# Layer 1's backward and output steps: SP in program order, z and x1 loads moved, squares written to SBUF

## The chip, the cores and the metric

One core of one Trainium2 chip runs the whole program. The metric is the device time of one execution in microseconds (us); the kernel before took 2016.53 us (median of three executions, 2014.89 to 2018.07). A change of 0.2%, some 4 us, is about what a measurement of this kernel can tell from none.

## What is computed

The reference is a two-layer backbone over 2048 latent tokens and 256 context tokens of width 1024. Layer 0 (chunked gating and windowed attention) is not touched. Layer 1 is a bidirectional gated linear recurrence and an output projection, followed by the final norm:

```python
z = depthwise_conv(xr, conv_w, conv_b)
for d, reverse in ((0, False), (1, True)):
    a_l, b_l = rglru_coeffs(z, w_a[d], b_a[d], w_i[d], b_i[d], lam[d])   # two sigmoid gates, exp, sqrt
    s_l = linear_scan(a_l, b_l, h0, reverse)
    h_lat = s_l if h_lat is None else h_lat + s_l
y = (h_lat * silu(g)) @ w_out
x = x + gate * y
return rmsnorm(x, final_g)
```

All products are made of three float32r products of high and low halves, so an operand is first split into such halves (on ScalarE and VectorE).

## The kernel before

The 18 tiles of 128 tokens go in 9 pairs (`L = NPAIR = 9`). Layer 1 is a software pipeline of steps `s` = 0 to 24, one call of `step(s)` each. A step does the recurrence work of one pair, which `gate(s)` names, in four blocks `b` of 256 channels, and the projection work of another pair, which `proj(s)` names, in four PSUM banks `b`:

- recurrence: forward direction in steps 3 to 11, backward direction in steps 12 to 20 (step 12 is the context pair, which stores no result);
- projection: `xr_mm` in steps 0 to 8, `g_mm` (the gate branch) in steps 9 to 16, `out_mm` (the output projection, the residual and the norm) in steps 17 to 24.

Within a step the order of ScalarE (ACT), TensorE (PE) and VectorE (DVE) is that of the code, since the loop stands in `tc.manual_schedule` for these three engines (L1422). GpSimd (POOL) and the sequencer SP, from which all DMAs are issued, are ordered by the scheduler, which emits what it finds ready.

The order of the code in a backward step `s`, as far as it matters:

1. `z_load(s)` (L1316): four loads `zf<-zs` of 256 KB, z of the next pair, into a ring of six buffers (L1206). Blocks 0 and 1 take buffers that the step before has done with. Blocks 2 and 3 take those of this step's own blocks 0 and 1, which POOL's product `ig<-ig,zf` (L1108) reads last.
2. `halves_load(s+1)`: four loads `op<-h1s` of 512 KB (until step 16).
3. for each block, `gmm` (PE, `pr` and `pig`) and `gates_act` (ACT sigmoids, L1106); between them the work left over from the step before (`tail`, which calls `post`) and `next_z(s, b)`: the split `zhl<-zf` of the next pair's z, ACT L84 and then DVE L87. Blocks 0 and 1 are split between the sigmoids, block 2 after all four and after `mm(0)`.
4. `coeff` (ACT L1125, DVE L1128 to L1132) of blocks 0 and 1, `next_z(s, 3)`, `mm(1)`, `coeff` of blocks 2 and 3, `root` (ACT L1136), `mm(2)`, `op_load(s+1, k)` (in steps 16 to 23, two loads of 512 KB).
5. `scan(d, i, (0, 1))`: DVE `r<-r,ig` (L1141), the scans (L1149), the sum with the forward result (L1158) and the product with the gate (L1160), then the store `y1s<-T` (L1164); `mm(3)`; `scan` of blocks 2 and 3 likewise.
6. `load_hg` (L1166): eight loads `hf<-hfs` and `gs<-gs` of 256 KB for the next pair's sums.

The sigmoid of block 0 writes the buffer of `r` that the scan of block 0 in the step before has read (ring of four). `hook` loads new weights `w<-kepto` of 1 MB each: the output weights `wo[2]` and `wo[3]` in step 17, behind `next_z(s, 2)`; banks 2 and 3 of that step need them.

In an output step, `post(b)` (L1230) adds the bank to the residual rows (DVE L1239) and takes the sum of squares on ACT, writing the squares back into the bank:

```python
dve.tensor_tensor(xt, xt, po, ALU.add)
act.activation(po, xt, AF.Square, accum_out=ss[:, half:half + 1])
if late:
    late.pop()()
```

so the bank is free for the next product when ACT L1240 is done. The residual rows `xt<-x1s` (256 KB a half) come into a ring of four buffers with the tag "gs", loaded in `post` when a tile's first half is met; the same buffers hold a tile's finished rows until the store `out<-xt` (`late`, L1266) has landed. `FG` rows, `og` and the ring "T" (four buffers of the scans) are the other buffers that the change names.

Of the kernel before, what the change touches and what calls it, by code (L numbers as in the profile page):

```python
# [7 lines left out]
F32 = mybir.dt.float32  # L8
F32R = mybir.dt.float32r
BF16 = mybir.dt.bfloat16  # L10
AF = mybir.ActivationFunctionType
# [4 lines left out]
P = 128  # L16
# [17 lines left out]
U_AT = 5  # L34
Y_ROWS = 1
T_PE = 14
MOD_AT = 8
WO1_AT = (2, 4, 6, 8, 10, 11, 12, 13)

# [2 lines left out]
def backbone_kernel(ctx: ExitStack, tc: tile.TileContext, a, out):  # L42
    nc = tc.nc
    pe, act, dve, pool, sp = nc.tensor, nc.scalar, nc.vector, nc.gpsimd, nc.sync
# [974 lines left out]
    L = NPAIR  # L1019
    order = [0] + list(range(L - 1, 0, -1))  # L1020

    with ExitStack() as c4:
# [185 lines left out]
        def g_mm(s, i, b):  # L1208
# [9 lines left out]

            return mm, post

        def out_mm(s, i, b):
            x, half = divmod(b, 2) if s > 2 * L - 1 else (b % 2, b // 2)
            t = 2 * i + x

            def mm():
                ps = px_tile()
                mm_wide(ps, wo[2 * half:2 * half + 2], lambda hl, c: ops[s, c][:, hl, x * P:(x + 1) * P])
                pxs[b] = ps

            def post():  # L1230
                if half == 0:
                    xts[t] = []
                    for h in range(2):
                        xt = b1.tile([P, 512], F32, tag="gs", name="xt", bufs=4)
                        sp.dma_start(xt, x1s[t][:, 512 * h:512 * h + 512])
                        xts[t].append(xt)
                    xts[t].append(b1.tile([P, 2], F32, tag="ss", name="ss", bufs=2))
                xt, ss, po = xts[t][half], xts[t][2], pxs.pop(b)
                dve.tensor_tensor(xt, xt, po, ALU.add)  # L1239
                act.activation(po, xt, AF.Square, accum_out=ss[:, half:half + 1])  # L1240
                if late:
                    late.pop()()
                end = s == 3 * L - 3 and x == 1
                if half == 0:
                    if end:
                        dve.tensor_tensor(xt, xt, FG[:, 0:512], ALU.mult)
                    return
                ms = b1.tile([P, 1], F32, tag="ms", name="ms", bufs=2)
                e = dve if end else pool
                if end:  # L1250
                    og = b1.tile([P, 512], F32, tag="G", name="og", bufs=1)
                    dve.tensor_tensor(og, xt, FG[:, 512:], ALU.mult)
                e.tensor_tensor(ms, ss[:, 0:1], ss[:, 1:2], ALU.add)
                e.tensor_scalar(ms, ms, 1.0 / D, EPS, ALU.mult, ALU.add)
                pool.tensor_tensor(ms, ms, mhalf[:, 0:1], ALU.pow)

                def final():
                    o = xts[t][:2]
                    if end:
                        o[1] = og  # L1260
                        act.activation(o[0], o[0], AF.Copy, scale=ms)
                        dve.tensor_scalar(og, og, ms, None, ALU.mult)
                    for h in range(2):
                        if not end:
                            dve.scalar_tensor_tensor(o[h], o[h], ms, FG[:, 512 * h:512 * h + 512], ALU.mult, ALU.mult)
                        sp.dma_start(out[0, (t - NCT) * P:(t - NCT + 1) * P, 512 * h:512 * h + 512], o[h])  # L1266

                late.append(final)

            return mm, post  # L1270
# [40 lines left out]
        def next_conv(s, b):  # L1311
            nx = gate(s + 1)
            if nx and nx[0] == 0:
                conv(nx[1], b)

        def z_load(s):  # L1316
            nx = gate(s + 1)
            if nx and nx[0]:
                for b in range(4):
                    sp.dma_start(z_tile(*nx, b), zs[nx[1]][:, 2 * b:2 * b + 2])  # L1320

        def step(s):
            g, M = gate(s), proj(s)

            def G(f, *args):
                if g:
                    f(*g, *args)
# [13 lines left out]
            def tail(b):  # L1341
                if len(tails) and tails[0][0] == b:
                    tails.pop(0)[1]()

            z_load(s)
            if s + 1 < 2 * L - 1:
                halves_load(s + 1)
            first = early(s) and s != 2 * L - 1
# [2 lines left out]
            G(gmm, 0)  # L1351
            G(gates_act, 0)
            tail(3)
            if early(s) and not first:
                op_split(s, 0)
            next_conv(s, 0)
            G(gmm, 1)
            G(gates_act, 1)
            if early(s):
                op_split(s, 1)  # L1360
            next_conv(s, 1)
# [32 lines left out]
            if source(s + 1) and s + 1 >= 2 * L - 1:  # L1394
                for k in range(2):
                    op_load(s + 1, k)
                    if not early(s + 1):
                        op_split(s + 1, k)
            if E:
                post(0)  # L1400
            G(scan, (0, 1))
# [14 lines left out]
        def early(s):  # L1416

            return 2 * L - 1 <= s <= 2 * L + 2
# [1 line left out]
        tails = []  # L1420
        step(0)
        with tc.manual_schedule(engines={mybir.EngineType.Activation, mybir.EngineType.PE, mybir.EngineType.DVE}):  # L1422
            for s in range(1, 3 * L - 2):
                step(s)
            for _, f in tails:
                f()
            late.pop()()
# [49 lines left out]
```

## Time and profile before

| | us |
|---|---|
| three executions, median (lowest to highest) | 2016.53 (2014.89 to 2018.07) |
| the profiled execution | 2019.23 |
| its span, first to last instruction | 2017.4 |
| matmuls busy in the span (PE) | 1903.2 (94%) |
| VectorE (DVE) busy | 1527.7 (76%) |
| ScalarE (ACT) busy | 1086.5 (54%) |
| GpSimd (POOL) busy | 619.8 (31%) |
| granted TensorE clock, mean | 0.974 |

PE is busy nearly all the time as a mean over the span, but the mean hides the stretch that the change touches: steps 12 to 24, which run from about 1571 us to the end. There the idle time of the weight loads (PEld) shows PE's waits, since matmuls are modelled as overlapping. A row of the timeline gives start, duration, engine, line, operation, tiles, count and in brackets the idle time of the engine before it with what ended it. "SPq" is the sequencer that issues DMAs: its duration is that of the issue, not of the transfer.

### The profile page before, as it was taken

Reading aid. Unit: us, or ns where it says so; the run is one execution under the profiler, and the core shown is the slowest. Engines: PE = TensorE matmul, PEld = TensorE weight load, DVE = VectorE, ACT = ScalarE, POOL = GpSimd, SP = SyncE. Lnnn points to the kernel's source line nnn. Section 1 sums busy time; section 2 is a strip of 40 time slices with the busy share of each in tenths; the row PEclk is TensorE's granted clock in tenths of the full one; section 3 lists DMA queues with packets and bytes.
Section 4 is the critical chain, followed back from the end, with each engine's and each line's share of the span. In section 5 each row is a group of like instructions: output and inputs, shape, how many; then the busy total and the mean of one; then the engine's idle time right before and its main releaser. Section 6 shows DMA issues by size and latency. Waiting matters only on the chain.

```text
span 2017.4 us, 33905 instructions
## 1 busy us (share of the span) xinstructions
PE 1903.2 (94%) x12159; PEld 1701.9 (84%) x12159; DVE 1527.7 (76%) x3223; ACT 1086.5 (54%) x2205; POOL 619.8 (31%) x801
## 2 busy tenths in 40 slices
PE   7999999999999899799989999999999999988998
PEld 3778888888887788688878889999999999877777
DVE  8878989786745787838888854798987566877863
ACT  6656656666655332323443551676767666756621
POOL 2745646454422311200010010443422121244310
PEclk8999999999999899899999999999999999988999
DMA  9355535352344897465555555324476464866442
GB/s 344 124 180 186 176 137 176 118 199 71 126 142 149 297 353 281 172 230 182 198 205 182 206 208 186 107 100 147 167 260 222 161 200 167 295 218 192 136 160 91
DMA packets 184788, 375.79 MB, mean 186 GB/s; under 512 B 18694, under 2 KB 78858, under 8 KB 176428
## 3 DMA queue, kind: packets, MB, share of 16 engines
q1 hardware_dynamic: 184620, 373.64, 53.0%
q8 instruction: 95, 1.56, 0.3%
q14 instruction: 73, 0.60, 0.1%
HBM read 246.41 MB, written 127.17 MB: 185 GB/s over the span
## 4 chain that ended last, share of the span: by engine, by line
PE 57%; DVE 19%; ACT 10%; DMA 7%; issue 6%; POOL 1%; SPq 1%; POOLq 0%; DVEq 0%; ACTq 0%
PE px L90 6%; PE px L92 6%; PE px L91 6%; DVE h1T L904 4%; PE pu L90 3%; PE pu L91 3%; PE pu L92 3%; PE po L573 3%; PE ptp L561 2%; DVE yT L904 2%; DVE macc L231 2%; ACT h1T L175 2%; DMA mraw<-in_w_mod 2%; PE pl L515 1%; PE pq L91 1%
## 5 line engine op out<-in xcount | busy, mean ns | idle before, releaser
L90 PE MATMUL px<-op,w 128*128 128x256 f32 x1088 | 308.1, 283 | 0.0
L91 PE MATMUL px<-op,w 128*128 128x256 f32 x1088 | 307.9, 283 | 0.0
L92 PE MATMUL px<-op,w 128*128 128x256 f32 x1088 | 307.9, 283 | 0.0
L91 PEld LDWEIGHTS px<-op,w 128*128 128x128 f32 x1088 | 208.9, 192 | 0.0
L90 PEld LDWEIGHTS px<-op,w 128*128 128x128 f32 x1088 | 208.9, 192 | 0.0
L92 PEld LDWEIGHTS px<-op,w 128*128 128x128 f32 x1088 | 208.9, 192 | 0.0
L543 POOL TENSOR_SCALAR s<-s,ri 128x640 f32<-128x640 f32 (+2 forms) x144 | 134.4, 947 | 97.1 <-DVE ri L540 93.0
L535 ACT ACTIVATE s<-s,mn 128x641 f32<-128x641 f32 (+2 forms) x144 | 113.3, 788 | 65.8 <-DVE mn L517 57.7
L84 ACT ACTIVATE pT<-ptp 128x512 fp32r<-128x512 f32 (+1 forms) x192 | 99.7, 536 | 89.5 <-PE ptp L561 86.4
L1108 POOL TENSOR_TENSOR ig<-ig,zf 128x512 f32<-128x512 f32 x72 | 109.9, 1534 | 98.0 <-ACT ig L1106 88.7
L87 DVE TENSOR_TENSOR zhl<-zf,zhl 128x512 fp32r<-128x512 f32 x72 | 60.2, 843 | 102.8 <-ACT zhl L84 102.7
L573 PE MATMUL po<-pT,v 128*128 128x256 f32 x656 | 130.1, 296 | 6.1 <-DVE pT L87 4.4
L87 DVE TENSOR_TENSOR pT<-ptp,pT 128x512 fp32r<-128x512 f32 (+1 forms) x192 | 114.4, 604 | 23.3 <-ACT pT L84 22.6
L90 PE MATMUL px<-w,op 128*128 128x512 f32 x256 | 103.5, 404 | 14.9 <-ACT px L1240 14.9
L573 PEld LDWEIGHTS po<-pT,v 128*128 128x128 f32 x656 | 98.5, 189 | 17.2 <-DVE pT L87 9.1
L175 ACT ACTIVATE h1T<-h1T,mc 128x128 f32<-128x128 f32 x112 | 44.7, 482 | 119.0 <-DVE h1T L904 119.0
L561 PE MATMUL ptp<-ident,s 128*128 128x128 f32 x656 | 104.0, 273 | 3.9 <-POOL s L543 2.1
L1152 POOL COPY carry<-T 128x2 f32<-128x2 f32 x68 | 34.7, 510 | 232.1 <-DVE T L1149 222.1
L904 DVE STREAM_TRANSPOSE h1T<-hrow 32x256 f32<-32x256 f32 x224 | 97.7, 436 | 8.1 <-ACT hrow L956 5.0
L91 PE MATMUL px<-w,op 128*128 128x512 f32 x256 | 102.5, 400 | 0.0
L92 PE MATMUL px<-w,op 128*128 128x512 f32 x256 | 102.4, 400 | 0.0
L517 DVE CUSTOM_DVE_ANT_0 s<-pl,mask,mn 128x384 f32<-128x384 f32 (+1 forms) x128 | 76.1, 594 | 31.5 <-PE pl L515 30.1
(280 smaller groups left out, 6237.4 us busy)
## 6 DMA issues: line engine op xcount, KB each, us to landing
hp<-h0s SPq DMA_DIRECT2D x45, 1024.0 KB
op<-h1s SPq DMA_DIRECT2D x64, 512.0 KB
mraw<-in_w_mod SPq DMA_DIRECT2D x48, 512.0 KB
h0s<-hT SPq DMA_DIRECT2D x18, 1024.0 KB
h1s<-h1hl SPq DMA_DIRECT2D x36, 512.0 KB
xt<-in_x SPq DMA_DIRECT2D x32, 512.0 KB
gs<-gs SPq DMA_DIRECT2D x64, 256.0 KB
raw<-in_ab_w_in SPq DMA_DIRECT2D x22, 512.0 KB
```

Source lines behind the costliest of these rows:

```text
L84: act.activation(hi, src, AF.Copy)
L87: (eng_lo or dve).tensor_tensor(lo, src, hi.bitcast(F32), ALU.subtract)
L90: pe.matmul(ps, lhsT=lhs(0), rhs=rhs(0), start=first, stop=False)
L91: pe.matmul(ps, lhsT=lhs(1), rhs=rhs(0), start=False, stop=False)
L92: pe.matmul(ps, lhsT=lhs(0), rhs=rhs(1), start=False, stop=last)
L175: act.activation(hT[:, o], tp[:, i], AF.Identity, scale=mc[:, 1, k, m:m + 1], bias=mc[:, 0, k, m:m + 1])
L535: act.activation(s[:, 0:nk], s[:, 0:nk], AF.Exp, scale=-1.0, bias=st["mn"][:, row, i:i + 1], accum_out=st["sm"][:, i:i + 1])
L543: pool.tensor_scalar(s[:, 1:nk], s[:, 1:nk], ri[:, i:i + 1], 0.0, ALU.mult, ALU.add)
L561: pe.transpose(tp[:, x, h], s_t[h][:, 1 + i * P:1 + (i + 1) * P], ident)
L573: pe.matmul(pos[t, g][:, 2 * P * e:2 * P * (e + 1)], lhsT=vl, rhs=pT[:, hl, x], start=i == 0 and hl == 0, stop=i == n - 1 and hl == 1)
L904: dve.transpose(out[o, :, s], src[s, :, o])
L1108: pool.tensor_tensor(res[1], res[1], zfs.pop((d, i, b)), ALU.mult)
```

## The change

Four edits, all in layer 1:

- steps 12 to 24 stand in a second `manual_schedule` block that names SP too, so the DMAs of these steps are issued in the order of the code;
- `z_load` takes block numbers. Blocks 0 and 1 for a step are now called a step earlier (before `post(0)` and the scans), block 2 after the first `gates_act`, block 3 after the second;
- the rows of x1 are loaded by `x1_load`, twice in step 17 after its first `gates_act`, and then each time a finished tile has been sent out by `late.pop()()`;
- the squares go to an SBUF tile `sq` (tag "G", one buffer) instead of back into the bank; `og` moves to the ring "T".

```diff
+BACK = 12
+        x1_next = [2 * i + x for i in order[1:] for x in range(2)]
+        def x1_load():
+            if x1_next:
+                t = x1_next.pop(0)
+                xts[t] = []
+                for h in range(2):
+                    xt = b1.tile([P, 512], F32, tag="gs", name="xt", bufs=4)
+                    sp.dma_start(xt, x1s[t][:, 512 * h:512 * h + 512])
+                    xts[t].append(xt)
+                xts[t].append(b1.tile([P, 2], F32, tag="ss", name="ss", bufs=2))
@@ out_mm, post @@
-                if half == 0:
-                    xts[t] = []
-                    ...
-                act.activation(po, xt, AF.Square, accum_out=ss[:, half:half + 1])
+                sq = b1.tile([P, 512], F32, tag="G", name="sq", bufs=1)
+                act.activation(sq, xt, AF.Square, accum_out=ss[:, half:half + 1])
                 if late:
                     late.pop()()
+                    x1_load()
-                    og = b1.tile([P, 512], F32, tag="G", name="og", bufs=1)
+                    og = b1.tile([P, 512], F32, tag="T", name="og", bufs=4)
-        def z_load(s):
+        def z_load(s, *bs_):
-                for b in range(4):
+                for b in bs_:
@@ step @@
-            z_load(s)
+            if s == L + 2:
+                z_load(s, 0, 1)
             ...
             G(gates_act, 0)
             tail(3)
+            if s == 2 * L - 1:
+                x1_load()
+                x1_load()
             ...
+            z_load(s, 2)
             G(gmm, 1)
             G(gates_act, 1)
+            z_load(s, 3)
             ...
+            if s > L + 1:
+                z_load(s + 1, 0, 1)
             if E:
                 post(0)
             G(scan, (0, 1))
@@ the loop @@
-            for s in range(1, 3 * L - 2):
+            for s in range(1, BACK):
+                step(s)
+        with tc.manual_schedule(engines={mybir.EngineType.Activation, mybir.EngineType.PE, mybir.EngineType.DVE,
+                                         mybir.EngineType.SP}):
+            for s in range(BACK, 3 * L - 2):
                 step(s)
```

## Rows read from the trace of the kernel before

**Rows 1.** Windows: us, busy time (instructions) by engine, granted clock, DMA share, GB/s.
```profile
1801.00:1843.00 42.00, 39.03 (x193) 34.16 (x194) 35.68 (x48) 26.11 (x58) 18.78 (x19) 0.85 0.56 176
```

**Rows 2.** Waits, 1560 to 1935 us: engine, line, awaited: total, times, longest us.
```profile
ACT zhl L84 <- DMA zf<-zs: 48.5, 7, 11.3
PEld px L90 <- ACT px L1240: 17.5, 6, 4.4
PEld pr L90 <- ACT r L1106: 17.0, 5, 7.2
```

**Rows 3.** Timeline, ACT: split of z's block 2 in steps 12 to 15, 17 to 19.
```profile
1592.79 0.63 ACT L84 ACTIVATE zhl<-zf 128x512 fp32r<-128x512 f32 x1 [8.38 <-DMA zf<-zs]
...
1623.69 0.63 ACT L84 ACTIVATE zhl<-zf 128x512 fp32r<-128x512 f32 x1 [3.70 <-DMA zf<-zs]
...
1663.99 0.63 ACT L84 ACTIVATE zhl<-zf 128x512 fp32r<-128x512 f32 x1 [9.45 <-DMA zf<-zs]
...
1703.68 0.63 ACT L84 ACTIVATE zhl<-zf 128x512 fp32r<-128x512 f32 x1 [10.99 <-DMA zf<-zs]
...
1783.13 0.63 ACT L84 ACTIVATE zhl<-zf 128x512 fp32r<-128x512 f32 x1 [11.25 <-DMA zf<-zs]
...
1819.86 0.64 ACT L84 ACTIVATE zhl<-zf 128x512 fp32r<-128x512 f32 x1
...
1860.22 0.63 ACT L84 ACTIVATE zhl<-zf 128x512 fp32r<-128x512 f32 x1
```

**Rows 4.** Timeline, DVE: last gate products of steps 13 to 18, first products of 15, 16.
```profile
1652.38 3.48 DVE L1160 SCALAR_TENSOR_TENSOR T<-T,gs 128x512 f32<-128x512 f32 x2
...
1692.68 3.48 DVE L1160 SCALAR_TENSOR_TENSOR T<-T,gs 128x512 f32<-128x512 f32 x2
...
1719.19 1.29 DVE L1141 TENSOR_TENSOR r<-r,ig 128x512 f32<-128x512 f32 x2
...
1733.61 3.48 DVE L1160 SCALAR_TENSOR_TENSOR T<-T,gs 128x512 f32<-128x512 f32 x2
...
1753.26 1.29 DVE L1141 TENSOR_TENSOR r<-r,ig 128x512 f32<-128x512 f32 x2
...
1772.44 2.37 DVE L1160 SCALAR_TENSOR_TENSOR T<-T,gs 128x512 f32<-128x512 f32 x2
...
1814.08 1.28 DVE L1160 SCALAR_TENSOR_TENSOR T<-T,gs 128x512 f32<-128x512 f32 x2
...
1854.43 1.28 DVE L1160 SCALAR_TENSOR_TENSOR T<-T,gs 128x512 f32<-128x512 f32 x2
```

**Rows 5.** Timeline, SP: issues at the start of step 15; a store and its buffer's load.
```profile
1687.83 4.14 SPq L1046 DMA_DIRECT2D op<-h1s  x4
...
1697.76 0.32 SPq L1320 DMA_DIRECT2D zf<-zs  x1
...
1823.12 1.00 SPq L1266 DMA_DIRECT2D out<-xt  x2
1826.44 0.97 SPq L1235 DMA_DIRECT2D xt<-x1s  x2
```

**Rows 6.** A window of dense transfers (columns as in 1); one load alone, issue and reader.
```profile
1756.00:1776.00 20.00, 20.00 (x131) 18.34 (x130) 19.90 (x24) 10.99 (x24) 13.41 (x8) 1.00 1.02 392
...
1944.33 1.01 SPq L1235 DMA_DIRECT2D xt<-x1s  x2
...
1947.06 0.69 DVE L1239 TENSOR_TENSOR xt<-xt,px 128x512 f32<-128x512 f32 x1 [3.50 <-DMA xt<-x1s]
```

**Rows 7.** Timeline: step 13's third gates on PE; step 18's third sigmoid on ACT.
```profile
1613.04 0.19 PEld L90 LDWEIGHTS pr<-zhl,w 128*128 128x128 f32 x1 [0.97 <-ACT r L1106]
...
1810.54 0.84 ACT L1106 ACTIVATE r<-pr,cv 128x256 f32<-128x256 f32 x2 [5.81 <-DVE T L1149]
```

**Rows 8.** Groups by line, 1560 to 1935 us: ACT writing 128x512 to SBUF and PSUM.
```profile
L1136 ACT ACTIVATE r<-r 128x512 f32<-128x512 f32 x40 | 21.9, 620 | 0.1
...
L1240 ACT ACTIVATE px<-xt 128x512 f32<-128x512 f32 x15 | 9.0, 599 | 34.4 <-DVE xt L1239 34.4
```

More of the change, by code (lines that the diff above doesn't have):

```diff
@@ L1230, in post @@
             def post():
-                if half == 0:
-                    xts[t] = []
[L1233 to L1237, printed above, removed]
                 xt, ss, po = xts[t][half], xts[t][2], pxs.pop(b)
                 dve.tensor_tensor(xt, xt, po, ALU.add)
-                act.activation(po, xt, AF.Square, accum_out=ss[:, half:half + 1])
+                sq = b1.tile([P, 512], F32, tag="G", name="sq", bufs=1)
+                act.activation(sq, xt, AF.Square, accum_out=ss[:, half:half + 1])
                 if late:
                     late.pop()()
+                    x1_load()
                 end = s == 3 * L - 3 and x == 1
```

## The prediction

> **What bounds the kernel now.** I read the windows of the last 450 us first, then the waits of that stretch, then ACT's, DVE's and SP's timelines around each wait. PE is the busiest engine, but in the touched steps it waits: of 42 us in one window its weight loads are busy 34.16 at a mean clock of 0.85 [rows 1]. The waits name two causes [rows 2]: 17.0 us for the sigmoids that empty the gate banks, 17.5 us for the squares that free an output bank. 34.5 us is thus all the idle time that can be won on PE.
>
> Behind the first cause stands a third wait: ACT waits 48.5 us for loads of z [rows 2]. The timeline of ACT shows where: at the split of block 2, by 8.38, 3.70, 9.45, 10.99 and 11.25 us in steps 12 to 15 and 17, and not at all in steps 18 and 19 [rows 3]; the two waits left, 4.7 us together, fall in step 16. ACT is in program order, so coefficients, roots, scans and the next step's sigmoids all stand behind that split. Blocks 0 and 1 are not waited for.
>
> In steps 13 to 15 this closes a loop that is longer than PE's step. Call F the end of a step's last gate product on DVE. F of steps 13, 14 and 15 is 1655.86, 1696.16 and 1737.09 (start plus duration), which is 40.3 and 40.9 us apart [rows 4]. The loop has three legs: F to the next step's block-2 split (1703.68 - 1696.16 = 7.5 us; 1663.99 - 1655.86 = 8.1 the step before), split to first product L1141 (1719.19 - 1703.68 = 15.5), and L1141 to F (1737.09 - 1719.19 = 17.9) [rows 3, 4]. What the change does to the first leg decides.
>
> **SP in program order and z moved.** Before, the scheduler issued the four `op` loads at 1687.83, well ahead of F, and z's block 2 at 1697.76, 1.6 us after F [rows 5]. In the code's order block 2 of z, called after the first `gates_act` of a step, stands behind everything that the step before still has to issue: the stores of `scan` of blocks 2 and 3, the last of which waits on DVE for F, then eight `load_hg` loads, then this step's four `op` loads and the last gate store. None of these needs to come before z, but a waiting store holds the whole queue. So the transfers that used to run before F now run after it, and ahead of z.
>
> The price of a transfer: a window of dense transfers moved 392 GB/s at a full DMA share [rows 6], so 256 KB (262144 bytes) take 0.67 us and 512 KB 1.34. A load alone took 1944.33 to 1947.06 = 2.7 us [rows 6]. After F: 0.5 us to the first `hg` issue, 2.7 until it lands, 7 x 0.67 for the others (7.9), 4 x 1.34 for `op` (13.3), 0.67 for the gate store and 0.67 for z: z lands at F + 14.6. Where no `op` loads stand between (into step 16) F + 9.2; into step 17 with four x1 halves ahead of it F + 11.9; into steps 18 and 19, without the gate store, F + 8.6. Bounds of the first: 12 (transfers begin before F's store is out, or overlap more) and 16 (0.77 us each, if stores slow the loads).
>
> The sum, step by step, as the time of block 2's split against [rows 3]:
> - Step 12 has no `hg` loads ahead of z (the context pair has no forward result to add), so its wait of 8.38 us goes. Step 13 then has z in time: its wait of 3.70 goes, and so does a 0.97 us stall of PE before it [rows 3, 7], and F of step 13 is 4.7 us earlier, 1651.2. I take all of it; the other end is none.
> - Step 14: 1651.2 + 14.6 = 1665.8, against 1663.99: 1.8 later.
> - Step 15: F 1698.0, z at 1712.6 against 1703.68: 8.9 later; F of step 15 is 1746.0.
> - Step 16: before, z was issued ahead of F and the first product began at 1753.26 [rows 4]. Now z lands at 1746.0 + 9.2 = 1755.2, the product follows 15.5 later at 1770.7: 17.4 later. F moves from 1774.81 to 1792.2.
> - Step 17: 1792.2 + 11.9 = 1804.1 against 1783.13: 21.0 later, F 1836.4 (before 1815.36).
> - Step 18: 1836.4 + 8.6 = 1845.0 against 1819.86: 25.1 later, F 1880.8 (before 1855.72).
> - Step 19: 1880.8 + 8.6 = 1889.4 against 1860.22: 29.2 later.
> Step 20 loads no z, and from there to the end the order is as before.
>
> Calling blocks 0 and 1 a step ahead gains nothing: nobody waited for them. SP is held in two more places. The weights `wo[2]`, `wo[3]` of step 17 now come behind F of step 16, x1 and z, four times 1 MB: F + 12 to F + 23, so PE stands in that step before its bank 2. The gates of step 18 begin later by that, but their third sigmoid waited for a scan on DVE until 1810.54, 27.4 us after block 2's split at 1783.13 [rows 3, 7]. That scan, now at F + 39, leaves 16 us after the last weight for two banks of products and the first gates, so it hides the weights and I cost them at nothing; if that cover fails, 3 us. A long idle of PE also lowers the granted clock, as the mean of 0.85 shows [rows 1]; off the loop, so nothing, or up to 4 us.
>
> **x1 ahead.** Before, the load of a tile's rows was issued when the stores of the tile that held its buffers had landed: stores at 1823.12, loads at 1826.44 [rows 5]. The ring still has four buffers, so `x1_load` waits for the same stores. Gain nothing; SP is held for those 2 to 3 us a tile, with loads and stores behind it that nobody needs within 5 us: cost nothing, 1 us at most.
>
> **Squares to SBUF.** The bank is free after DVE L1239 instead of after ACT L1240, so 0.6 us (599 ns, [rows 8]) earlier at each of six waits, 17.5 us in all [rows 2]. But what PE waits for is DVE, which is late because of the loop; only the last of the six counts on the path: 0.6 us won, bounds 0 and 3.6. The square itself: ACT took 599 ns into PSUM and 620 into SBUF for this shape [rows 8], 0.02 us each, three in a step: nothing. The Trainium skill, page "ScalarE: Activation LUTs", section "Step-by-step: what each stage is for", speaks against this edit, ScalarE being faster into PSUM than into SBUF; the rows agree in sign, and 32 times 0.02 us changes the sum by 0.7 us at the very most.
>
> Sum: 29.2 - 0.6 = 28.6 us. The profiled execution took 2019.23, 1.8 more than its span and 2.7 more than the median; against it 2047.8, against the median of 2016.53 **2045.1**, say 2045. With the first leg at 12 (and 7.6, 10 and 7.2 for the others) and 3.6 us for the banks the same steps give +14 and 2030; with 16 (10.2, 13.3, 9.7) and no gain in step 13, +41 and 2058.
>
> **Rivals.**
> 1. *z lands in time.* The place is the first leg: the rival holds if block 2 lands less than 7.5 us after F. Then the loads of a step are wanted late enough to hide. The five stalls of 17.0 us [rows 2] go, plus 0.6 for the bank: about 1999. For it: the transfers ahead of z are needed only 25 us later, the queue is idle for much of each step. Against it: the order of the code. The Trainium skill, page "DMA: Bandwidth & Descriptors", section "Rules for kernel authors", has this rival's rule: issue a DMA early and wait for it late. By that rule the time would fall; the trace bears it out for blocks 0 and 1 alone, which have nothing to win. The skill's "Perfetto Trace Analysis", section "DMA Optimizations", suggests keeping loads and stores on separate engines, which is the forecast's side: here a load stands behind a store that waits; no trace here shows the two apart.
> 2. *The order hardly changes, or gains and losses meet:* the early steps win 4.7 to 8.4 us, PE's own work hides the rest until step 16, and the weights and x1 cost nothing. Between 2012 and 2020.
> 3. *More than z:* the covers fail too, 3 us for the weights, 4 for the clock and 1 for x1 on top of the upper bound: 2060 and more.
>
> **How the numbers follow.** Forecast 0.71, rival 1 0.14, rival 2 0.09, rival 3 0.06. Time 2045. Faster by over 0.2% (what a measurement here can tell from nothing) 0.14, within 0.09, slower 0.77. The range takes the forecast's bounds to 2058 and goes down over rival 2 to 2012, leaving out rival 1 and rival 3, 0.20.
>
> **What would show it.** Right: SP issues eight `hg`, four `op`, a `gs` and then `zf` in one run that begins at F; ACT's wait for `zf` is gone in step 12, small in 13, and 12 us or more in steps 14 to 17, new in 18 and 19; its total exceeds 48.5 us; F to F in steps 14 to 16 is near 47 us; `w<-kepto` for step 17 is issued behind `zf`, and PE waits for it. The waits for L1240 become waits for L1239. Wrong: `zf` issued ahead of `hg`, or the wait of block 2 under 5 us in steps 14 to 17; then rival 1.

## The result, and the profile after

| us | before | after |
|---|---|---|
| executions on one chip, median (lowest to highest) | 2016.89 (2014.89 to 2018.07) | 2064.46 (2061.82 to 2070.68) |
| ratio to before, 95% interval | | 1.0242 (1.0224 to 1.0259) |
| the profiled execution's span | 2017.4 | 2068.9 |
| granted TensorE clock, mean | 0.974 | 0.963 |

The change costs 47.6 us; 28.6 were forecast, with 2058 as the upper end. The sign and the mechanism are as forecast, the size is not. A later series of the changed kernel gave 1.0261 (1.0247 to 1.0275). The profiled execution of the changed kernel is the longest of its five (2070.68 us), so the spans differ by more, 51.5 us, than the medians.

The waits of the changed kernel from 1560 us on (engine, line, awaited: total, times, longest us) answer to [rows 2]:

```profile
ACT zhl L85 <- DMA zf<-zs: 83.1, 8, 20.9
...
PEld pr L91 <- ACT r L1107: 49.6, 6, 14.1
...
ACT op L85 <- DMA opr<-y1s: 28.8, 5, 8.0
...
PE px L91 <- DMA w<-kepto: 12.5, 2, 11.7
...
PEld px L91 <- DVE xt L1245: 6.5, 5, 2.4
```

ACT's wait for z grew from 48.5 to 83.1 us, and PE's wait for the sigmoids from 17.0 to 49.6. The 17.5 us of waits for the squares are gone; what is left of them, 6.5 us, is for the addition on DVE. Two rows are new: the op loads of the output steps (`opr`) and the weights.

SP's timeline at the end of step 14 (start, time of the issue, line, what) shows the order:

```profile
1702.64 2.00 SPq L1165 DMA_DIRECT2D y1s<-T  x2
1704.69 0.42 SPq L1171 DMA_DIRECT2D hf<-hfs  x1
...
1708.27 0.65 SPq L1171 DMA_DIRECT2D gs<-gs  x1
1709.02 4.01 SPq L1047 DMA_DIRECT2D op<-h1s  x4
1713.12 2.25 SPq L1218 DMA_DIRECT2D gs<-gs  x1
1715.46 1.91 SPq L1328 DMA_DIRECT2D zf<-zs  x2
```

The last y1s store is issued at F, then eight loads of the forward result and the gate ("hg"), four op loads, a gate store, and then z. Before, op was issued ahead of F and z's block 2 right behind it [rows 5].

ACT's timeline at the split of z's block 2, steps 12 to 19, answers to [rows 3]:

```profile
1584.64 0.63 ACT L85 ACTIVATE zhl<-zf 128x512 fp32r<-128x512 f32 x1 [0.26 <-DMA zf<-zs]
...
1621.51 0.63 ACT L85 ACTIVATE zhl<-zf 128x512 fp32r<-128x512 f32 x1 [2.56 <-DMA zf<-zs]
...
1671.39 0.63 ACT L85 ACTIVATE zhl<-zf 128x512 fp32r<-128x512 f32 x1 [17.88 <-DMA zf<-zs]
...
1722.74 0.63 ACT L85 ACTIVATE zhl<-zf 128x512 fp32r<-128x512 f32 x1 [20.87 <-DMA zf<-zs]
...
1767.69 0.63 ACT L85 ACTIVATE zhl<-zf 128x512 fp32r<-128x512 f32 x1 [14.48 <-DMA zf<-zs]
...
1817.98 0.63 ACT L85 ACTIVATE zhl<-zf 128x512 fp32r<-128x512 f32 x1 [16.08 <-DMA zf<-zs]
...
1859.36 0.63 ACT L85 ACTIVATE zhl<-zf 128x512 fp32r<-128x512 f32 x1 [4.18 <-DMA zf<-zs]
...
1906.61 0.63 ACT L85 ACTIVATE zhl<-zf 128x512 fp32r<-128x512 f32 x1 [6.79 <-DMA zf<-zs]
```

The wait of step 12 is gone (0.26 for 8.38 us) and that of step 13 is small; every later one is longer than before, and steps 18 and 19, which had none, have one. Against [rows 3] the split comes 8.2 and 2.2 us earlier in steps 12 and 13, then 7.4, 19.1, 34.9 (step 17), 39.5 and 46.4 us later.

DVE's timeline, last gate products of steps 13 to 18, gives F (start plus duration) and answers to [rows 4]:

```profile
1650.19 3.48 DVE L1161 SCALAR_TENSOR_TENSOR T<-T,gs 128x512 f32<-128x512 f32 x2
...
1701.87 2.38 DVE L1161 SCALAR_TENSOR_TENSOR T<-T,gs 128x512 f32<-128x512 f32 x2
...
1753.21 2.38 DVE L1161 SCALAR_TENSOR_TENSOR T<-T,gs 128x512 f32<-128x512 f32 x2
...
1798.88 3.48 DVE L1161 SCALAR_TENSOR_TENSOR T<-T,gs 128x512 f32<-128x512 f32 x2
...
1844.82 3.48 DVE L1161 SCALAR_TENSOR_TENSOR T<-T,gs 128x512 f32<-128x512 f32 x2
...
1890.58 3.47 DVE L1161 SCALAR_TENSOR_TENSOR T<-T,gs 128x512 f32<-128x512 f32 x2
```

F to F is now 50.6, 51.3, 46.8, 45.9 and 45.8 us, where it was 40.3 and 40.9 in steps 13 to 15. Two stretches of the span, from step 12's split to step 19's and from there to the end, say where the 51.5 us of span went (windows: us, busy time and instructions by engine, granted clock, DMA share, GB/s). The changed kernel:

```profile
1584.64:1906.61 321.97, 267.88 (x1881) 254.43 (x1880) 202.36 (x281) 174.95 (x352) 76.81 (x74) 0.90 0.51 172
1906.61:2068.90 162.29, 135.12 (x607) 111.41 (x606) 90.26 (x136) 60.90 (x134) 29.12 (x53) 0.93 0.41 140
```

The kernel before, whose first stretch begins where ACT begins to wait for step 12's split:

```profile
1584.41:1860.22 275.81, 254.27 (x1846) 243.13 (x1845) 200.43 (x281) 173.95 (x353) 79.34 (x74) 0.95 0.61 206
1860.22:2017.40 157.18, 141.14 (x645) 116.64 (x643) 93.49 (x138) 60.06 (x136) 32.30 (x54) 0.97 0.39 131
```

46.2 us arose up to step 19 (29.2 were forecast by the same two points, 1889.4 less 1584.4 against 275.8) and 5.1 in the output steps behind it, where nothing but the 0.6 us gain was forecast. In the trace of the later series this last stretch took 159.7 us, not 162.3, so 2.5 of the 5.1 are seen there.

### The profile page after: what moved, and what is told of

Same layout as the page of the kernel before. It is cut to its first block, busy times and chain, and to the rows that moved or that the text cites. A ratio compares the mean times of both kernels' runs of the same rounds, so it can differ in the third digit from the quotient of the medians.

```text
span 2068.9 us, 33913 instructions
## 1 busy us (share of the span) xinstructions
PE 1910.9 (92%) x12159; PEld 1708.9 (83%) x12159; DVE 1525.8 (74%) x3223; ACT 1088.1 (53%) x2205; POOL 618.4 (30%) x801
## 5 line engine op out<-in xcount | busy, mean ns | idle before, releaser
L88 DVE TENSOR_TENSOR zhl<-zf,zhl 128x512 fp32r<-128x512 f32 x72 | 65.5, 916 | 145.8 <-ACT zhl L85 128.3
L1109 POOL TENSOR_TENSOR ig<-ig,zf 128x512 f32<-128x512 f32 x72 | 105.3, 1465 | 115.8 <-ACT ig L1107 105.6
L88 DVE TENSOR_TENSOR pT<-ptp,pT 128x512 fp32r<-128x512 f32 (+1 forms) x192 | 114.3, 603 | 23.4 <-ACT pT L85 22.9
L91 PE MATMUL pr<-zhl,w 128*128 128x256 f32 x288 | 85.6, 297 | 48.4 <-ACT r L1107 48.4
L1153 POOL COPY carry<-T 128x2 f32<-128x2 f32 x68 | 34.7, 510 | 271.9 <-DVE T L1150 271.5
```

Source lines behind the costliest of these rows:

```text
L88: (eng_lo or dve).tensor_tensor(lo, src, hi.bitcast(F32), ALU.subtract)
L91: pe.matmul(ps, lhsT=lhs(0), rhs=rhs(0), start=first, stop=False)
L1109: pool.tensor_tensor(res[1], res[1], zfs.pop((d, i, b)), ALU.mult)
```

## The experiments

Theory A: the loss comes from SP's queue in program order, with z behind F and the loads that follow it; B: from the new places of the loads of z and x1 by themselves; C: from the squares; D and E stand with their runs. Ratios are to the kernel before on the same chip, with a 95% interval; the changed kernel stands at 1.0242 and, in the second series, 1.0261. 0.001 is 2.0 us.

| run | median us | ratio (interval) |
|---|---|---|
| changed, SP's order undone | 2019.19 | 1.0019 (1.0009 to 1.0028) |
| before, SP's order alone | 2082.10 | 1.0336 (1.0319 to 1.0353) |
| before, squares alone | 2015.75 | 0.9995 (0.9984 to 1.0006) |
| changed, hg and op behind z | 2011.42 | 0.9981 (0.9969 to 0.9993) |
| changed, op behind z | 2056.02 | 1.0205 (1.0177 to 1.0232) |
| changed, hg behind z | 2028.16 | 1.0068 (1.0044 to 1.0092) |
| changed, four of eight hg ahead of F | 2045.58 | 1.0148 (1.0126 to 1.0169) |
| changed, stores behind hg | 2074.47 | 1.0295 (1.0281 to 1.0309) |
| changed, output steps' op loads first | 2061.06 and 2064.71 | 1.0224 (1.0199 to 1.0249), 1.0244 (1.0230 to 1.0258) |
| changed, weights early | 2077.62 | 1.0310 (1.0290 to 1.0329) |
| changed, x1 as before | 2090.59 | 1.0371 (1.0356 to 1.0387) |
| hg and op behind z, output steps' op first | 2009.84 | 0.9968 (0.9955 to 0.9980) |
| the same, with weights and step 17's op early | 2006.09 | 0.9955 (0.9939 to 0.9970) |

### Which edit makes the loss

SP taken out of the second block again:

```diff
-        with tc.manual_schedule(engines={... Activation, ... PE, ... DVE, ... SP}):
+        with tc.manual_schedule(engines={... Activation, ... PE, ... DVE}):
             for s in range(BACK, 3 * L - 2):
```

> The changed kernel with one edit undone: SP is taken out of the second hand-ordered block, so the scheduler orders the DMAs again; the moved calls of z and x1 and the squares in SBUF stay. Theory A (the order of SP's queue alone makes the loss: z's blocks 2 and 3 stand behind the last y1s store, eight hg loads and four op loads): 2010 to 2020 us, that is the kernel before less about 0.6 us for the squares; ACT's wait for z in steps 13 to 19 returns to some 50 us from 83. Theory B (the new places of the z and x1 loads cost by themselves, whatever the order of the queue): still 2040 us or more. Theory C (the squares in SBUF cost): still over 2025.

1.0019, and ACT waits 48.0 us for z (48.5 before). So the loss needs SP's order: B and C cannot make it by themselves. With the scheduler's order the other edits together cost 2 to 6 us; which of them does, stays open.

SP's order alone, in the kernel before:

```diff
-            for s in range(1, 3 * L - 2):
+            for s in range(1, BACK):
                 step(s)
+        with tc.manual_schedule(engines={... Activation, ... PE, ... DVE, ... SP}):
+            for s in range(BACK, 3 * L - 2):
+                step(s)
```

> The kernel before with one edit done: SP named in a second hand-ordered block from step 12 on; z is loaded by four loads at the head of a step (so behind hg, but ahead of the four op loads), x1 where a tile's first half is met, squares in the bank. Theory A: slower than before, by less than the whole change, since in steps 14 and 15 the op loads (four of 1.3 us) no longer stand ahead of z: 64 (changed kernel's median 2064) less two times 5 us less 3 us of x1 in step 17, plus two times 1.3 us for z's blocks 0 and 1 ahead of block 2 in steps 18 and 19: 2050 to 2060 us. Theory B: within 0.3% of before, 2011 to 2023.

1.0336: over the upper end of 2060, and not less than the whole change but 19 us more. B falls again, since no call is moved here. Where the 19 us lie is read from F on DVE; the first row is the split of z's block 0 (not 2) on ACT, the others give F of steps 13 and 16:

```profile
1707.03 0.63 ACT L85 ACTIVATE zhl<-zf 128x512 fp32r<-128x512 f32 x1 [20.14 <-DMA zf<-zs]
...
1646.64 2.37 DVE L1161 SCALAR_TENSOR_TENSOR T<-T,gs 128x512 f32<-128x512 f32 x2
...
1786.23 3.45 DVE L1161 SCALAR_TENSOR_TENSOR T<-T,gs 128x512 f32<-128x512 f32 x2
```

With all four loads of z at the head of a step, block 0 stands behind hg as well, and its split is in ACT's order ahead of the sigmoids of blocks 2 and 3; so ACT waits there in place of block 2. But that is not where the time goes. From F of step 13 to F of step 16 this run takes 140.7 us and the changed kernel 148.7: without op ahead of z these steps are shorter, as was expected. From F of step 16 to the end of the span it takes 290.8 us and the changed kernel 266.5. In that stretch x1 is loaded where it is needed, and the run that undoes only x1's early call (below) takes 286.2 there. So the late x1 loads can account for most of the 19 us, and no gain from calling z's blocks 0 and 1 a step ahead is seen.

The squares alone:

```diff
-                act.activation(po, xt, AF.Square, accum_out=ss[:, half:half + 1])
+                sq = b1.tile([P, 512], F32, tag="G", name="sq", bufs=1)
+                act.activation(sq, xt, AF.Square, accum_out=ss[:, half:half + 1])
```

> The kernel before with one edit done: squares to an SBUF tile, og in the ring T. Theory A: 0 to 1 us faster than before, 2015.5 to 2017. Theory C (the squares cost): 2025 or more. If the bank's waits of 17.5 us were on the path: 2000 to 2013.

0.9995, between 3.2 us faster and 1.2 slower: C falls, and so does a large gain.

### What stands ahead of z

hg and op behind z's block 3:

```diff
             z_load(s, 3)
+            if s >= BACK and g and g[0] and g[1]:
+                for b in range(4):
+                    load_hg(g[1], b)
+            if s >= BACK and s + 1 < 2 * L - 1:
+                halves_load(s + 1)
@@ and the same calls at the end and the head of a step left out @@
```

> The changed kernel with SP still in program order, but the eight hg loads and the four op loads of a step called behind its z block 3 instead of ahead of z. Theory A: z's block 2 then waits for F and for the POOL product that frees its buffer only; it lands 5 to 6 us after F instead of 11 to 18, earlier than in the kernel before (7.5). What is left is PE's own time and the op loads of the output steps that stand behind out and x1 (about 5 us): 2002 to 2014 us. Theory B (the loss is in the output steps, the weights and x1, z only an accompaniment): 2045 to 2064. If hg is now late, the sum on DVE waits for hf and the gain is smaller, 2020 to 2035.

0.9981, as theory A said: 53 us less than the changed kernel, from the order of twelve loads alone. ACT's timeline at block 2 in steps 14 to 17:

```profile
1652.11 0.63 ACT L85 ACTIVATE zhl<-zf 128x512 fp32r<-128x512 f32 x1 [1.02 <-DMA zf<-zs]
...
1688.16 0.63 ACT L85 ACTIVATE zhl<-zf 128x512 fp32r<-128x512 f32 x1 [2.52 <-DMA zf<-zs]
...
1724.79 0.63 ACT L85 ACTIVATE zhl<-zf 128x512 fp32r<-128x512 f32 x1 [4.58 <-DMA zf<-zs]
...
1768.48 0.63 ACT L85 ACTIVATE zhl<-zf 128x512 fp32r<-128x512 f32 x1 [9.48 <-DMA zf<-zs]
```

The loop is broken: the splits of steps 14 to 16 stand 36.1 and 36.6 us apart. F of steps 13 and 14 is 1647.46 and 1683.18, so z's first leg is 4.7 and 5.0 us (17.7 and 18.5 in the changed kernel, 8.1 and 7.5 before). In step 17 four x1 loads stand ahead of z.

Then one of the two groups at a time, first op behind z:

```diff
-            if s + 1 < 2 * L - 1:
+            if s < BACK and s + 1 < 2 * L - 1:
                 halves_load(s + 1)
@@ behind z_load(s, 3) @@
+            if s >= BACK and s + 1 < 2 * L - 1:
+                halves_load(s + 1)
```

> The changed kernel with one edit: the four op loads of steps 13 to 16 called behind z's block 3, the eight hg loads still ahead of z. Theory A (each load ahead of z costs its transfer time): z's block 2 comes 4 x 1.3 = 5.2 us earlier in steps 14 and 15, so 2052 to 2056 us. If a load ahead of z cost nothing and the waiting store alone did: 2062 to 2066.

The first legs of steps 14 and 15 measure 12.3 and 12.6 us (F 1650.26 and 1694.68, splits 1662.52 and 1707.33), 5.4 and 5.9 less: four loads of 1.3 us each, as worked out. The time is 7.5 us less by the ratios, not the 11 of the two legs, and the intervals just overlap with the changed kernel's.

hg behind z (the four hg calls moved as above, op left ahead):

> The changed kernel with one edit: the eight hg loads called behind z's block 3, the four op loads still ahead of z. Theory A: the first load behind F lands after 4.4 us, three more of 1.3 us each, then the gate store and z, so z's block 2 comes about 10 us after F in steps 14 and 15 (18 in the changed kernel, 7.5 before), and 5 to 6 us after F from step 16 on: 2013 to 2022 us. If the waiting store alone cost (and not the loads behind it): 2055 or more.

35 us less than the changed kernel, so the loads of hg are the greater part. But 2028 is above what was expected: the first leg of steps 14 and 15 is 12.0 us, twice, not 10 (F 1646.32 and 1690.47, splits 1658.30 and 1702.47). A burst of op loads behind F is late as well: by the prediction's price it takes 9.2 us (0.5, then 2.7 and 0.67 for the first load of 512 KB, 1.34 for each of three more, 0.67 each for gs and z), so it is 2.8 us over, against 3.1 and 3.4 with hg alone ahead of z (12.3 and 12.6 for 9.2).

### The size of the first leg

Four of the eight hg loads ahead of F:

```diff
             G(scan, (0, 1))
+            n = gate(s + 1)
+            if n and n[0] and n[1]:
+                for b in range(2):
+                    load_hg(n[1], b)
             mm(3)
@@ at the end of the step @@
-                for b in range(4):
+                for b in range(2, 4):
                     load_hg(n[1], b)
```

> The changed kernel with one edit: four of the eight hg loads (blocks 0 and 1) are called right behind the scan of blocks 0 and 1, so they run ahead of F; four stay ahead of z. It tells what the slow start of the burst behind F is. Theory A1 (the first loads behind F are slow whatever their number, each further one costs its 0.65 us): z comes 4 x 0.65 = 2.6 us earlier in steps 14 to 19, 2046 to 2052 us. Theory A2 (the extra time grows with the burst, eight loads taking 11 us instead of 8): 5.5 us a step, 2028 to 2036. Theory A3 (only z's place behind the store counts): 2062 to 2066.

2045.58, 19 us less and just under A1's range. The first legs of steps 14 and 15 are 14.3 and 14.7 us, so four loads fewer give 3.4 and 3.8 us: somewhat more than 2.6 (A1) and well short of 5.5 (A2). By the prediction's price this leg is 11.9 us, so it is 2.4 and 2.8 us over, where the whole burst was 3.1 and 3.9 over. Most of the excess does not depend on how many loads follow. A3 falls. With z ahead of hg and op, where only a gate store stands between F and z, the leg is 0.8 and 1.1 us over (4.7 and 5.0 for 3.9).

Part of the excess shows in the rate. Windows of 2 us of the changed kernel, from the first hg load behind F of step 14 on (last column GB/s, ahead of it the DMA share):

```profile
1704.69:1706.69 2.00, 2.00 (x19) 2.00 (x19) 1.36 (x3) 0.00 (x0) 0.00 (x0) 1.00 0.86 202
1706.69:1708.69 2.00, 2.00 (x19) 2.00 (x18) 0.00 (x0) 0.00 (x0) 0.00 (x0) 1.00 0.81 162
1708.69:1710.69 2.00, 2.00 (x19) 2.00 (x18) 0.00 (x0) 0.00 (x0) 0.00 (x0) 1.00 0.87 246
1710.69:1712.69 2.00, 2.00 (x19) 2.00 (x19) 0.00 (x0) 0.00 (x0) 0.00 (x0) 1.00 1.04 374
```

In its first 6 us the burst moves 202, 162 and 246 GB/s, 1.22 MB in all, though the DMA engines are busy 81 to 87% of the time; only then 374. At the prediction's price (2.7 us for the first load, then 392 GB/s) these bytes take 5.1 us, so the slow start makes some 0.9 of the 3.9 us by which the leg into step 15 is over. Another 0.7 us, by the same rate, is a store that the price left out: up to 1722.69 5.25 MB are moved, and the loads ahead of z, z's two blocks and the gate store are 4.98 MB, so one y1s store of 256 KB was still running. These are estimates from the windows; the rest of the 3.9 us lies in the later windows, at 361 GB/s over the next 8 us and 287 over the last 4, and is not told apart. Whether the two stores in flight at F cause the slow start was tried by putting them behind hg:

```diff
+            if hg_next and i:
+                sp.dma_start(y1s[i][:, 6:8, 0:32], ris[d, i, 3][2][:, :, 0:32])
+            if hg_next:
+                for b in range(4):
+                    load_hg(hg_next, b)
             for b in bs_:
                 T = ris.pop((d, i, b))[2]
+                q = 32 if hg_next and b == 3 else 0
                 if i:
-                    sp.dma_start((y1s if d else hfs)[i][:, 2 * b:2 * b + 2], T)
+                    sp.dma_start((y1s if d else hfs)[i][:, 2 * b:2 * b + 2, q:], T[:, :, q:])
```

> The changed kernel with one edit: at F only a small part (32 of 256 columns) of the last y1s store is issued, then the eight hg loads, then the store of block 2 and the rest of block 3; the same bytes stand ahead of z, and 1.3 us of store more. Theory A4 (the two stores in flight slow the first loads): the first hg load lands 2.7 us after its issue and the eighth 7.4, z 14 to 16 us after F in steps 14 and 15: 2045 to 2060 us. Theory A5 (a burst of loads starts slowly by itself, stores or not): first landing again over 4 us or the gaps behind it over 1 us, z 18 to 20 us after F, 2063 to 2075.

2074.47, and first legs of 19.5 and 18.8 us, as A5 said. The same windows, from the first hg load of step 14 on:

```profile
1704.09:1706.09 2.00, 2.00 (x19) 2.00 (x19) 1.28 (x3) 0.00 (x0) 0.00 (x0) 1.00 0.51 97
1706.09:1708.09 2.00, 2.00 (x19) 2.00 (x18) 0.00 (x0) 0.00 (x0) 0.00 (x0) 1.00 0.99 171
1708.09:1710.09 2.00, 2.00 (x19) 2.00 (x18) 0.00 (x0) 0.00 (x0) 0.00 (x0) 1.00 0.84 297
1710.09:1712.09 2.00, 2.00 (x19) 2.00 (x19) 0.00 (x0) 0.00 (x0) 0.00 (x0) 1.00 1.06 410
```

With all but a small store gone from in front, the burst still starts at 97, 171 and 297 GB/s, so the two stores of 256 KB are not needed for it. The small store is no clean absence, though: its rows are of 128 bytes, and between 1703.6 and 1723.6 us 544 packets under 512 bytes are moved, 272 in the changed kernel between 1704 and 1724. A burst behind F with no store at all ahead of it was not tried, and the cause stays open.

### The covers: op, weights, x1

A cover is other work that was to hide a wait.

The op loads of the output steps ahead of out and x1:

```diff
             z_load(s, 3)
+            if s >= 2 * L - 1 and source(s + 1):
+                for k in range(2):
+                    op_load(s + 1, k)
@@ behind the roots @@
-                    op_load(s + 1, k)
+                    if s < 2 * L - 1:
+                        op_load(s + 1, k)
```

> The changed kernel with one edit: in the output steps the two op loads of the next step are called behind z's block 3, before any out store or x1 load of that step, instead of behind the roots; all else as changed. Theory A with its second term (about 5 us of the loss in steps 20 to 22 are op loads held behind an out store's landing and the x1 loads): 2057 to 2061 us against the changed kernel's 2064, and the waits of ACT for opr (28.8 us there) mostly gone. If the op loads cost nothing: 2063 to 2066.

> The changed kernel with the op loads of the output steps ahead of out and x1, once more in five rounds: by the second term of theory A 3 to 6 us below its partner on the same chip; if the op loads cost nothing, within 1 us of it.

> The changed kernel as it is, once more, as the partner of the next one on this chip: 2060 to 2070 us.

1.0224 against 1.0242, and 1.0244 against 1.0261 beside its partner of the same chip: 3.6 and 3.4 us less by the ratios, the same twice, but the intervals overlap each time. In the traces ACT's wait for opr falls from 27.0 to 10.2 us, and the stretch from step 19's split to the end from 159.7 to 156.7 (2061.5 - 1901.85 against 2059.2 - 1902.54). What held the loads is seen in SP's timeline of the changed kernel:

```profile
1947.45 1.01 SPq L1274 DMA_DIRECT2D out<-xt  x2
1954.32 0.95 SPq L1230 DMA_DIRECT2D xt<-x1s  x2
1955.33 0.90 SPq L1053 DMA_DIRECT2D opr<-y1s  x2
...
1981.04 1.00 SPq L1274 DMA_DIRECT2D out<-xt  x2
1983.10 1.13 SPq L1230 DMA_DIRECT2D xt<-x1s  x2
1984.28 0.90 SPq L1053 DMA_DIRECT2D opr<-y1s  x2
```

and in ACT's, where the op splits wait for them:

```profile
1961.34 2.38 ACT L85 ACTIVATE op<-opr 128x512 fp32r<-128x512 f32 x4 [1.06 <-DMA opr<-y1s]
...
1991.07 2.39 ACT L85 ACTIVATE op<-opr 128x512 fp32r<-128x512 f32 x4 [7.97 <-DMA opr<-y1s]
```

The first out stores are issued behind the hg loads, the x1 loads come 6.9 us after them since they take the same buffers and wait for their landing, and op, which needs none of these buffers, waits behind x1. That costs ACT only 1.06 us. The longest wait, 7.97 us, stands behind out stores that are issued at 1981.04, when DVE has finished the tile, and x1 loads 2.1 us behind those. So the term exists; its size, 3.0 us between these two traces, is not told from zero by the times.

The weights earlier:

```diff
-            hooks[s + 1, "z3"] = [(kind, 2, 0), (kind, 2, 1)]
-            hooks[s + 1, "c0"] = [(kind, 3, 0), (kind, 3, 1)]
+            late_w = [(kind, 2, 0), (kind, 2, 1)], [(kind, 3, 0), (kind, 3, 1)]
+            if kind == "g":
+                hooks[s + 1, "z3"], hooks[s + 1, "c0"] = late_w
+            else:
+                hooks[s, "m3"] = late_w[0] + late_w[1]
@@ step @@
             mm(3)
+            hook("m3")
```

> The changed kernel with one edit: the weights wo[2] and wo[3] are called behind the last bank of step 16, ahead of that step's last stores, instead of in step 17 behind F, x1 and z. Theory A (z's loop decides until step 19, so PE's 12 us for these weights is hidden): 2060 to 2066 us. Theory D (the cover fails, PE's wait for weights is on the path): 2050 to 2056.

Slower than the changed kernel, 1.0310, which no theory had. PE's wait for weights is gone, but four transfers of 1 MB now run just ahead of hg and z. SP's timeline in step 16:

```profile
1789.11 5.15 SPq L135 DMA_DIRECT2D w<-kepto  x4
```

ACT's split of block 2 in step 17:

```profile
1820.85 0.63 ACT L85 ACTIVATE zhl<-zf 128x512 fp32r<-128x512 f32 x1 [20.75 <-DMA zf<-zs]
```

F of step 16 is 1800.17 there, so that first leg is 20.7 us (15.6 in the changed kernel), and the sigmoids of step 18 are late in turn: PE waits 12.35 us for them at 1838.75. So the run tells of the queue once more and nothing clean about the cover: D is not shown, and whether PE's 12 us in step 17 are on the path of the changed kernel stays open. The changed kernel's own trace speaks for the cover as far as step 18: ACT stands at block 2's split there 4.18 us before z has landed, and F of step 17, which is ahead of that z in the queue, came 30.3 us after its split (32.2 before).

x1 as before, loaded when a tile's first half is met:

```diff
             def post():
+                if half == 0:
+                    x1_load()
                 xt, ss, po = xts[t][half], xts[t][2], pxs.pop(b)
                 ...
                     late.pop()()
-                    x1_load()
@@ step @@
-            if s == 2 * L - 1:
-                x1_load()
-                x1_load()
```

> The changed kernel with one edit undone: a tile's x1 rows are loaded in post when its first half is met, with SP still in program order. Theory A as predicted (x1 ahead gains and costs nothing, 1 us at most): 2062 to 2066 us. Theory E (in program order the early load hides the landing of x1, which DVE would else wait for at every tile): 2070 to 2085. If the x1 loads behind the out stores are what holds the op loads: 2057 to 2061.

26 us slower than the changed kernel, more than theory E's upper end of 2085. SP's timeline in steps 17 and 18:

```profile
1840.92 11.59 SPq L1165 DMA_DIRECT2D y1s<-T  x4
...
1856.78 0.96 SPq L1329 DMA_DIRECT2D zf<-zs  x2
1857.93 1.68 SPq L1230 DMA_DIRECT2D xt<-x1s  x2
```

DVE's, at F of step 16 (the end of this row is 1804.00) and at the addition that needs the last of these loads:

```profile
1800.53 3.47 DVE L1161 SCALAR_TENSOR_TENSOR T<-T,gs 128x512 f32<-128x512 f32 x2
...
1865.46 1.28 DVE L1247 TENSOR_TENSOR xt<-xt,px 128x512 f32<-128x512 f32 x2 [12.12 <-DMA xt<-x1s]
```

In program order a load called where it is needed stands behind the stores at F, hg and z; DVE, in order too, waits 12.12 us for it.

### Put together

z first, and the output steps' op loads ahead of out and x1:

> z's blocks 2 and 3 ahead of hg and op, and the op loads of the output steps behind those and ahead of out and x1. Theory A: the kernel with z first alone (2011.4) less some 5 us: 2004 to 2009. If the op loads are not on the path: 2010 to 2013.

On top of it the weights behind step 16's last bank, step 17's op loads ahead of them, and the first x1 loads behind z:

> Built on z first and op loads ahead of out and x1 (2009.8): the weights wo[2] and wo[3] are called behind the last bank of step 16, ahead of that step's last stores, the op loads of step 17 before the weights of step 16, and the first x1 loads of step 17 behind z and hg. Theory A: PE's waits for weights (8.3 and 1.6 us) and for the op splits of step 17 (4.7 us) go, as far as no other wait stands close behind them: 1996 to 2005 us. If these waits are off the path: 2008 to 2012.

0.9968 and 0.9955 against 0.9981 for z first alone: each step goes the expected way by about 3 us, none is told from the one before by its interval, and both medians are just over the upper end of what was expected. The last, 2006.1 us, beats both kernels: 9 us (6 to 12) less than before. Here the weights do no harm. That this is because z and hg no longer stand in one run behind F is argued, not shown.

## Why the prediction was right in kind and wrong in size

**The order of the queue: right.** SP's rows show the run of y1s, hg, op, gs, z as it was worked out, and the runs with SP's order undone and with z first take the loss away. The wait of step 12 goes, that of step 13 nearly does; ACT waits 12 us or more in steps 14 to 17, and steps 18 and 19 have a new wait. `w<-kepto` is issued behind z. F to F in steps 14 to 16 was named as near 47 us; it is 51.3 and 46.8. That the second nearly meets is luck: its leg was 2.9 us longer than forecast and the way from the split to F 2.3 us shorter.

**The price of a transfer behind F: the step that failed.** The leg was built of 2.7 us for a load alone and 0.67 for each further one, from a load in a quiet queue and from a window in full flow [rows 6]. The burst behind F is neither: it moves 162 to 246 GB/s for its first 6 us, and a store of 256 KB that the price left out still runs in front of it. By the estimate above these two make some 1.6 of the 3.9 us in the leg into step 15; the rest lies in lower rates later on and is not told apart.

| first leg into step | forecast us | measured us |
|---|---|---|
| 14 | 14.6 | 17.7 |
| 15 | 14.6 | 18.5 |
| 16 | 9.2 | 12.1 |
| 17 | 11.9 | 15.6 |
| 18 | 8.6 | 11.1 |
| 19 | 8.6 | 12.6 |

(Block 2's split less F.) That is 20.1 us too little in six legs, and the upper bound of 16 us for the first, 0.77 us a load, was too low as well: it raised the price of each load and left the start alone. The other differences nearly meet: step 13's split 2.5 us later than said, the way from split to F 5.3 us shorter in all (34.7 for 37.0 us in step 16, 30.3 for 32.3 in step 17). 20.1 + 2.5 - 5.3 = 17.3 of the 17.2 us by which step 19's split came later than the 1889.4 forecast.

**op loads at nothing: wrong by some 3 us in the traces.** The prediction named SP's wait of 2 to 3 us a tile and said that nobody needs what is behind it within 5 us. ACT did: it waited 28.8 us for `opr`, where x1 was issued up to 6.9 us behind out, and out itself behind a burst of hg or behind DVE, and op was behind both. Taking op ahead shortened the output steps by 3.0 us in the traces; the times do not tell this from zero. With 17.2 us up to step 19's split, the 5.1 us behind it (2.5 in the other trace) and the 0.6 not seen, the 22.9 us between the forecast span (2017.4 + 28.6) and the measured one add up.

**x1 ahead, "gain nothing": right against the kernel before, wrong inside the change.** With the scheduler's order the moved calls gain nothing (1.0019). In program order x1's early call is worth 26 us. Even so DVE waits 13.9 us in all for x1 (5.2 before), which the prediction did not have; no run tells whether this is on the path. The Trainium skill, page "DMA: Bandwidth & Descriptors", section "Rules for kernel authors", says to issue a DMA early and wait for it late; x1's move follows it, and the runs agree (2090.59 us without it, 2064.46 with). Rival 1 took that rule for z's block 2 too, but there the call was early in no sense that counts: it stood behind F.

**z's blocks 0 and 1 a step ahead, "gains nothing": nothing here speaks against it.** SP's order with all of z at the head of a step and x1 late stands at 1.0336, the changed kernel with x1 late at 1.0371. The first has z ahead of op, which the run with op behind z puts at 7.5 us, so no gain of the early call is seen, and its own price is not known.

**Weights at nothing: not decided.** PE stood 12 us for them, as the prediction expected. The cover held as far as step 18's split, where z came last; behind that it could not be tested apart.

**The clock at nothing: not separated.** It fell from 0.95 to 0.90 in the first stretch, where the loop and not PE decides, and from 0.97 to 0.93 in the output steps, where it may be part of the 5.1 us. The prediction's "up to 4 us" has no row behind it, and no run here shows it.

**Squares 0.6 us: right as far as it can be told** (between 3.2 us gained and 1.2 lost). The waits for the squares became shorter waits for the addition.

**The rivals.** Rivals 1 and 2 are out. The time fell where rival 3 put it, over 2060, but the larger part is not its reasons, the covers: 17.2 of the 22.9 us missing in the span lie up to step 19's split, where the forecast's own term was too small. What the weights and the clock add is not decided.

## What to carry to other kernels

When a DMA queue is put in program order, write down per step what stands ahead of each load and which store, waiting for which engine, is ahead of that; the load on the loop goes first behind the store, what is needed 20 us later goes behind it. Here that order alone is 53 us. A load that must wait for a store to land should not stand ahead of one whose buffer is free: here that took ACT's waits from 27.0 to 10.2 us, though the gain in time is not told from zero. For the time of a load behind a burst, take a like burst in the trace from its first issue to its last landing, with the stores still running ahead of it, and not the rate of its full flow.

## What the hardware showed that was not expected

A burst of 256 KB loads starts at about half its later rate: 202, 162, 246 and then 374 GB/s in windows of 2 us, with DMA shares of 0.86, 0.81, 0.87 and 1.04. The engines are thus busy while they move little. In the bursts of the steps before and after, from 1654.10 and 1755.97 us on, it is 141, 196, 310, 341 and 210, 180, 289, 363. It is so with two stores of 256 KB ahead of the burst and with only a small store of short rows ahead of it (97, 171, 297, 410). A burst that begins with 512 KB loads recovers sooner (194, 317, 299, 368 from 1690.95 us on, in the run with hg behind z), yet its first leg was late as well, 12.0 for 9.2 us. No run here tells why.
